# Attention work issued one product at a time between the large products, and one reciprocal per head

## The chip, the cores and the metric

The kernel runs on one core of one Trainium2 chip. The metric is the device time of one execution in microseconds (us). Several executions are timed, and one more is recorded by the hardware profiler.

## What is computed

Two transformer blocks on one sequence of 512 tokens with 1024 features, all in f32. The first block mixes sparse attention (8 heads of 64 in two groups; each has a selected, a window and a compressed branch) with retention (4 heads of 128). The second has an mLSTM layer (8 heads of 128) and a forgetting-attention layer (16 heads of 64), each with a convolutional feed-forward part.

```python
# sparse attention, one block of queries
sc = einsum('qghd,cgd->gqhc', qi, k_cmp) * scale
p_c = softmax(where(valid, sc, NEG));  o_c = einsum('gqhc,cgd->qghd', p_c, v_cmp)
p_s = softmax(where(smask, ss, NEG));  o_s = einsum('gqhk,gqkd->qghd', p_s, v_sel)
p_w = softmax(where(wmask, sw, NEG));  o_w = einsum('gqhk,kgd->qghd', p_w, v_win)
o = gi[..., 0:1] * o_c + gi[..., 1:2] * o_s + gi[..., 2:3] * o_w
# retention, one chunk
inner = einsum('bhnm,bhme->bhne', einsum('bhnd,bhmd->bhnm', qc, kc) * dmat, vc)
# mLSTM, one chunk
s = einsum('bhtd,bhsd->bhts', qt, kt) * exp(dmat - m_t[..., None])
num = einsum('bhts,bhse->bhte', s, vt) + ...
# forgetting attention
logits = einsum('bqhd,bkhd->bhqk', qi, k) + (ci[..., :, None] - c[..., None, :])
p = softmax(where(mask, logits, -inf));  o = einsum('bhqk,bkhd->bqhd', p, v)
```

All of it is causal. Around these stand the projections `h @ w_in`, `h @ w_up` and their like, whose weights are far larger than the activations.

## The kernel before

**Large products.** Each f32 operand of a projection is cut into a high and a low part, and `mm3` (L474) issues three products per weight tile of 128x128: high by high, high by low, low by high, mostly 512 columns wide. `gemm` and `gemm_tok` loop over the eight row blocks and call `mm3`, or issue the same three products themselves (L582 to L584). The weights come by DMA, are split by ScalarE (L169) and VectorE (L171), and are held in four buffers of each part.

**Attention as filling.** Four stages put attention work between the large products of a projection that does not depend on it: sparse attention, retention, mLSTM and forgetting attention. The work is written as generators. Each step issues some instructions and then yields a number, its written cost in ns. A filler holds a credit: `tick(ns)` after some large products adds `ns` times the stage's ratio, and steps are taken from the generator while the credit is above zero:

```python
    def tick(self, ns):
        self.credit += ns * self.ratio
        while self.gen is not None and self.credit > 0:
            try:
                self.credit -= next(self.gen)
...
def pipeline(items):
    n = len(items)
    for s in range(n + 2):
        yield from weave(*(items[s - d][d]() for d in range(3) if 0 <= s - d < n and items[s - d][d]))
```

An item is one head (of one branch). It has three parts, and in step `s` the pipeline weaves the first part of item `s`, the second of item `s - 1` and the third of item `s - 2`, one yield of each in turn; one such turn is called a round here. In the two softmax stages the parts are:

1. `score_steps` (L849): for each of four blocks of 128 queries, two score products of 128 to 512 columns into a bank of PSUM (the tile `s`, two buffers), with a mask product in the forgetting attention; then a reduction on VectorE (L862), the exponential with the row sum on ScalarE (L864), a reciprocal (L866) and a scaling (L868, L870) on VectorE. The result is a tile `P`.
2. `transpose_steps` (L874): ten transposes of 128x128 (L880), gathered in one bank (the tile `t`, one buffer) for each of four blocks of keys, and a copy by ScalarE (L882) to a tile `PT`.
3. `av` (L936, L1608), once for two heads: for each block of keys, the product of values and `PT` of either head (L939, L1613), 512, 384, 256 and 128 columns wide. The first head writes partitions 0 to 63 of the tile `o`, the second 64 to 127. The two products of one block are called a couple here.

The compressed branch has parts of the same kind with small tiles (`cmp_scores`, `cmp_transposes`, `avc`). Retention has `ret_scores`, `ret_out`, `ret_norm`, the mLSTM `m_scores`, `m_out`, `m_norm`; their products of weights and values have 128 output rows.

**What sets the order on each engine.** The framework's planner orders the whole program. Each engine gets, by the planner's own cost estimates, the instruction written earliest among those whose operands and buffers it deems ready. So the written order is a priority and not the order of execution: a later large product can run ahead of a transpose whose input isn't ready. On the chip each engine then keeps that order and waits on semaphores.

Of the kernel before, what the change touches and what calls it, by code (L numbers as in the profile page):

```python
# [194 lines left out]
def block_kernel(ctx: ExitStack, tc: tile.TileContext, I, out):  # L195
# [278 lines left out]
    def mm3(ps, w, a, first, last):  # L474
        (h, l), (ah, al) = w, a
        T.matmul(ps, lhsT=h, rhs=R(ah), start=first, stop=False)  # L476
        T.matmul(ps, lhsT=h, rhs=R(al), start=False, stop=False)  # L477
        T.matmul(ps, lhsT=l, rhs=R(ah), start=False, stop=last)  # L478

# [19 lines left out]
    def gemm(acts, nb, evac, lead=0, mid=None, halves=False, rest=None):  # L499
# [6 lines left out]
        b = 0  # L506
        if lead:
# [5 lines left out]
            for ts in thalf if halves else (slice(0, 512),):  # L513
                for k in range(KT):
                    for c in range(2 * lead):
                        mm3(ps[c][:, ts], cut(w[c // 2][k], c % 2), [t[:, ts] for t in acts[k]], k == 0, k == KT - 1)
                        if c % 2:
                            tick(1280)
# [6 lines left out]
        while b < nb:  # L525
            if KT <= 8:
                w = WT.get()
                for c in range(2):
                    ps = g_bank()
                    with in_order(tc, (mybir.EngineType.PE,)) if rest else nullcontext():  # L530
                        for k in range(KT):
                            mm3(ps, cut(w[k], c), acts[k], k == 0, k == KT - 1)
                            if k % 2:
                                tick(1280)
# [4 lines left out]
            else:  # L539
                ps = [g_bank(), g_bank()]  # L540
                for k0 in range(0, KT, 8):
                    w = WT.get()
                    for k in range(len(w)):
                        for c in range(2):
                            mm3(ps[c], cut(w[k], c), acts[k0 + k], k0 + k == 0, k0 + k == KT - 1)
                        tick(1280)
# [22 lines left out]
    def gemm_tok(acts, cols, evac, then=None, rest=None):  # L569
# [3 lines left out]
        with in_order(tc, (mybir.EngineType.PE,)) if rest else nullcontext():  # L573
            for k0 in (0, 4):
                w = WT.get()
                for k in range(4):
                    ah, al = acts[k0 + k]
                    h, l = w[k]
                    for i in range(4):
                        ts = slice(i * 128, (i + 1) * 128)  # L580
                        first, last = (k0 + k == 0), (k0 + k == 7)
                        T.matmul(ps[i][:, 0:cols], lhsT=R(ah)[:, ts], rhs=h, start=first, stop=False)  # L582
                        T.matmul(ps[i][:, 0:cols], lhsT=R(al)[:, ts], rhs=h, start=False, stop=False)  # L583
                        T.matmul(ps[i][:, 0:cols], lhsT=R(ah)[:, ts], rhs=l, start=False, stop=last)  # L584
                        if i % 2:
                            tick(1280)
# [235 lines left out]
    kcS = []  # L822
# [26 lines left out]
    def score_steps(P, g, q, k, cb, scale_cols):  # L849


        for i in range(4):
# [3 lines left out]
            T.matmul(ps[:, 0:L], lhsT=R(q[g][:, c]), rhs=R(k[0][g][:, 0:L]), start=True, stop=False)  # L856
            T.matmul(ps[:, 0:L], lhsT=R(q[g][:, c]), rhs=R(k[1][g][:, 0:L]), start=False, stop=cb is None)  # L857
            if cb is not None:
                T.matmul(ps[:, L - 128:L], lhsT=R(identr), rhs=R(maskr), start=False, stop=True)
            pr = unit("P")  # L860
            mx, rs = small(1, "mx"), small(1, "rs")
            V.tensor_tensor_reduce(out=pr[:, 0:L], in0=ps[:, 0:L], in1=cdiag[:, 512 - L:512] if cb is None else cb[:, 0:L],  # L862
                                   scale=1.0, scalar=3e38, op0=OP.add, op1=OP.min, accum_out=mx)
            A.activation(pr[:, 0:L], pr[:, 0:L], AF.Exp, scale=-1.0, bias=mx, accum_out=rs)  # L864
            rr = small(1, "rr")
            V.reciprocal(rr, rs)  # L866
            if scale_cols is None:
                V.tensor_scalar(pr[:, 0:L], pr[:, 0:L], rr, None, op0=OP.mult)  # L868
            else:
                V.tensor_scalar(pr[:, 0:L], pr[:, 0:L], rr, scale_cols[i], op0=OP.mult, op1=OP.mult)  # L870
            P.append(pr)
            yield 210 * (i + 1) + 60

    def transpose_steps(P, PT):  # L874

        yield from wait(1)
# [824 lines left out]
```

## Time and profile before

| | |
|---|---|
| three timed runs | 2171.95, 2175.36, 2176.06 us; median 2175.36 |
| the profiled execution | 2174.73 us, its span 2173.0 us |
| mean granted TensorE clock | 0.994 of full speed |
| busy: TensorE, its weight loads, VectorE, ScalarE, GpSimd | 97%, 79%, 57%, 43%, 16% of the span |
| the four stages, us from the span's start | sparse attention 97 to 271, retention 271 to 357, mLSTM 920 to 1026, forgetting attention 1564 to 1725 |

The span runs from the first to the last instruction of the profiled execution. In the rows, PE is TensorE's matmul, PEld its weight load, DVE VectorE, ACT ScalarE, POOL GpSimd, SP SyncE. `L880` is line 880 of the kernel. A record `t<-ident,P 128*128 128x128` writes the tile `t` from the tiles `ident` and `P`; the shape behind the names is that of the stationary operand, and the last one is the moving operand. Matmul records overlap, since they are pipelined, so what one costs is read from the step between starts. An f32 product with values has two records, one for each pass.

### The profile page before, as it was taken

The numbers are of one execution on the slowest core, as the hardware profiler recorded it, in microseconds if no ns is written. First come the engines' busy times: TensorE is split into PE (matmuls) and PEld (weight loads), VectorE is DVE, ScalarE is ACT, GpSimd is POOL, SyncE is SP. The second block draws the span as 40 slices with busy tenths as digits, with TensorE's granted clock in tenths as the row PEclk, the third lists the DMA queues.
The fourth block names the chain that finished last, engine by engine and source line by source line (L and its number), as shares of the span: only waits on it lengthen the run. The fifth ranks groups of instructions, "written<-read, shape, count | busy, mean of one in ns | idle before, by whom it ended". The sixth has DMA issues, their size and how long they took to land.

```text
span 2173.0 us, 26666 instructions
## 1 busy us (share of the span) xinstructions
PE 2116.9 (97%) x10314; PEld 1709.2 (79%) x10314; DVE 1240.5 (57%) x2247; ACT 943.2 (43%) x1638; POOL 341.0 (16%) x351
## 2 busy tenths in 40 slices
PE   7899999999999999999999999999999999999998
PEld 6766678887888888987888888889866788888887
DVE  7876545644333334867696664256477559666422
ACT  5666433344313424555364443234466536444322
POOL 5421000002101201320221110021121022111000
PEclk9999999999999999999999999999999999999999
DMA  6321122432233222422423332223322142333222
GB/s 162 106 77 58 40 63 82 128 97 78 97 97 93 89 90 79 134 91 73 131 78 97 97 97 87 80 87 126 118 70 66 57 129 78 97 97 97 88 74 72
DMA packets 242031, 198.75 MB, mean 91 GB/s; under 512 B 15182, under 2 KB 232986, under 8 KB 241904
## 3 DMA queue, kind: packets, MB, share of 16 engines
q1 hardware_dynamic: 237808, 186.11, 28.2%
q0 software_dynamic: 4096, 10.94, 1.6%
q8 instruction: 81, 1.33, 0.3%
q14 instruction: 46, 0.38, 0.1%
HBM read 190.69 MB, written 6.34 MB: 91 GB/s over the span
## 4 chain that ended last, share of the span: by engine, by line
PE 85%; DVE 5%; ACT 2%; issue 1%; DMA 0%; DVEq 0%; ACTq 0%; POOLq 0%; POOL 0%
PE g L476 24%; PE g L477 24%; PE g L478 24%; PE g L582 2%; PE g L584 2%; PE g L583 2%; PE t L880 1%; PE o L1613 1%; PE o L939 1%; PE s L856 1%; DVE wl L171 1%; PE s L857 1%; DVE x L1415 1%; PE t L1300 0%; PE o L1034 0%
## 5 line engine op out<-in xcount | busy, mean ns | idle before, releaser
L476 PE MATMUL g<-hi,wh 128*128 128x512 f32 (+1 forms) x2604 | 1005.4, 387 | 6.1 <-DVE gates L749 5.4
L477 PE MATMUL g<-lo,wh 128*128 128x512 f32 (+1 forms) x2604 | 994.9, 382 | 7.3 <-DVE lo L1420 7.3
L478 PE MATMUL g<-hi,wl 128*128 128x512 f32 (+1 forms) x2604 | 995.1, 382 | 3.6 <-POOL wl L171 1.9
L171 DVE TENSOR_TENSOR wl<-raw,wh 128x1024 fp32r<-128x1024 f32 (+4 forms) x337 | 405.5, 1205 | 399.4 <-ACT wh L169 398.6
L476 PEld LDWEIGHTS g<-hi,wh 128*128 128x128 f32 x2604 | 493.0, 190 | 115.4 <-issue 14.0
L169 ACT ACTIVATE wh<-raw 128x1024 fp32r<-128x1024 f32 (+3 forms) x348 | 355.9, 1025 | 521.8 <-PE g L477 452.6
L477 PEld LDWEIGHTS g<-lo,wh 128*128 128x128 f32 x2604 | 493.3, 189 | 104.5 <-DVE lo L1420 8.2
L478 PEld LDWEIGHTS g<-hi,wl 128*128 128x128 f32 x2604 | 493.2, 189 | 102.9 <-DVE wl L171 3.1
L864 ACT ACTIVATE P<-P,mx 128x128 f32<-128x128 f32 (+3 forms) x128 | 71.9, 561 | 47.4 <-DVE mx L862 46.1
L582 PE MATMUL g<-wh,hi 128*128 128x384 f32 (+3 forms) x256 | 85.4, 334 | 0.1
L584 PE MATMUL g<-wl,hi 128*128 128x384 f32 (+3 forms) x256 | 84.2, 329 | 0.0
L583 PE MATMUL g<-wh,lo 128*128 128x384 f32 (+3 forms) x256 | 84.1, 329 | 0.0
L882 ACT COPY PT<-t 128x512 f32<-128x512 f32 (+3 forms) x128 | 53.7, 420 | 53.4 <-PE t L880 52.4
L1133 POOL TENSOR_TENSOR relu<-relu 128x512 f32<-128x512 f32 x32 | 40.9, 1281 | 212.7 <-ACT relu L1132 207.5
L880 PE MATMUL t<-ident,P 128*128 128x128 f32 x320 | 65.2, 284 | 3.7 <-ACT PT L882 1.3
L880 PEld LDWEIGHTS t<-ident,P 128*128 128x128 f32 x320 | 38.7, 140 | 32.5 <-ACT PT L882 20.2
L1379 POOL TENSOR_TENSOR sq<-sq 128x512 f32<-128x512 f32 x16 | 27.1, 1694 | 229.4 <-ACT sq L1373 228.8
L374 DVE TENSOR_TENSOR lo<-relu,hi 128x512 fp32r<-128x512 f32 x32 | 21.9, 691 | 71.1 <-ACT hi L373 71.1
L582 PEld LDWEIGHTS g<-wh,hi 128*128 128x128 f32 x256 | 48.2, 188 | 4.4 <-issue 2.8
L454 POOL TENSOR_TENSOR sq<-sq 128x512 f32<-128x512 f32 x12 | 18.0, 1501 | 207.5 <-ACT sq L450 202.5
L866 DVE RECIPROCAL rr<-rs 128x1 f32<-128x1 f32 x128 | 20.5, 160 | 51.4 <-ACT P L864 50.9
L856 PE MATMUL s<-ks,qs 128*128 128x128 f32 (+3 forms) x128 | 46.9, 369 | 2.9 <-DVE mx L862 2.5
(926 smaller groups left out, 2222.4 us busy)
## 6 DMA issues: line engine op xcount, KB each, us to landing
raw<-in_ffn_w_up_dram SPq DMA_DIRECT2D x88, 512.0 KB, 4.9
raw<-in_w_in_dram SPq DMA_DIRECT2D x16, 1024.0 KB, 5.1
raw<-in_w_up_dram SPq DMA_DIRECT2D x16, 1024.0 KB, 5.4
raw<-in_w_down_dram SPq DMA_DIRECT2D x16, 1024.0 KB, 4.9
raw<-in_ffn_w_down_dram SPq DMA_DIRECT2D x12, 1024.0 KB, 5.0
raw<-in_mlstm_w_in_dram SPq DMA_DIRECT2D x8, 1024.0 KB, 5.3
raw<-in_fox_w_qg_dram SPq DMA_DIRECT2D x8, 1024.0 KB, 5.2
raw<-in_ffn_w_down_dram SPq DMA_DIRECT2D x6, 768.0 KB, 4.3
```

The lines of the kernel that those rows point to most:

```text
L169: self.nc.scalar.activation(h[:, 0:b - a].bitcast(F32R), raw[:, a:b], AF.Copy)
L171: e.tensor_tensor(l[:, 0:b - a].bitcast(F32R), raw[:, a:b], h[:, 0:b - a], op=OP.subtract)
L476: T.matmul(ps, lhsT=h, rhs=R(ah), start=first, stop=False)
L477: T.matmul(ps, lhsT=h, rhs=R(al), start=False, stop=False)
L478: T.matmul(ps, lhsT=l, rhs=R(ah), start=False, stop=last)
L582: T.matmul(ps[i][:, 0:cols], lhsT=R(ah)[:, ts], rhs=h, start=first, stop=False)
L583: T.matmul(ps[i][:, 0:cols], lhsT=R(al)[:, ts], rhs=h, start=False, stop=False)
L584: T.matmul(ps[i][:, 0:cols], lhsT=R(ah)[:, ts], rhs=l, start=False, stop=last)
L856: T.matmul(ps[:, 0:L], lhsT=R(q[g][:, c]), rhs=R(k[0][g][:, 0:L]), start=True, stop=False)
L864: A.activation(pr[:, 0:L], pr[:, 0:L], AF.Exp, scale=-1.0, bias=mx, accum_out=rs)
L880: T.transpose(pt[:, i * 128:(i + 1) * 128], P[i][:, j * 128:(j + 1) * 128], ident)
L882: A.copy(t[:, j * 128:512], pt[:, j * 128:512])
```

## The change

The credit is given after every single product of 512 columns, or in proportion for narrower ones, instead of after every six. Every step of the generators yields after nearly every product, with new written costs, and the four ratios are new. In `score_steps` the four row sums of a head go to one tile of four columns; one reciprocal serves all of them, the gate is multiplied into it in the sparse attention, and the four scalings follow at the end of the head. `transpose_steps` lets three rounds pass where it let one pass. The compressed branch's last part yields until the compressed values have been written (`vc_done`).

```diff
@@ -474,8 +474,11 @@
     def mm3(ps, w, a, first, last):
         (h, l), (ah, al) = w, a
         T.matmul(ps, lhsT=h, rhs=R(ah), start=first, stop=False)
+        tick(230)
         T.matmul(ps, lhsT=h, rhs=R(al), start=False, stop=False)
+        tick(230)
         T.matmul(ps, lhsT=l, rhs=R(ah), start=False, stop=last)
+        tick(230)
...
@@ -514,8 +517,6 @@
                 for k in range(KT):
                     for c in range(2 * lead):
                         mm3(ps[c][:, ts], cut(w[c // 2][k], c % 2), [t[:, ts] for t in acts[k]], k == 0, k == KT - 1)
-                        if c % 2:
-                            tick(1280)
...
-                            if k % 2:
-                                tick(1280)
...
-                        tick(1280)
...
-                        T.matmul(ps[i][:, 0:cols], lhsT=R(ah)[:, ts], rhs=h, start=first, stop=False)
-                        T.matmul(ps[i][:, 0:cols], lhsT=R(al)[:, ts], rhs=h, start=False, stop=False)
-                        T.matmul(ps[i][:, 0:cols], lhsT=R(ah)[:, ts], rhs=l, start=False, stop=last)
-                        if i % 2:
-                            tick(1280)
+                        for a, w_, f, e in ((ah, h, first, False), (al, h, False, False), (ah, l, False, last)):
+                            T.matmul(ps[i][:, 0:cols], lhsT=R(a)[:, ts], rhs=w_, start=f, stop=e)
+                            tick(0.45 * cols)
...
-    kcS = []
+    kcS, vc_done = [], []
...
+        rs = small(4, "rs")
         for i in range(4):
             L = 128 * (i + 1)
             ps = s_bank()
             c = slice(i * 128, (i + 1) * 128)
             T.matmul(ps[:, 0:L], lhsT=R(q[g][:, c]), rhs=R(k[0][g][:, 0:L]), start=True, stop=False)
+            yield 58 * (i + 1)
             T.matmul(ps[:, 0:L], lhsT=R(q[g][:, c]), rhs=R(k[1][g][:, 0:L]), start=False, stop=cb is None)
+            yield 58 * (i + 1)
             if cb is not None:
                 T.matmul(ps[:, L - 128:L], lhsT=R(identr), rhs=R(maskr), start=False, stop=True)
             pr = unit("P")
-            mx, rs = small(1, "mx"), small(1, "rs")
+            mx = small(1, "mx")
             V.tensor_tensor_reduce(out=pr[:, 0:L], in0=ps[:, 0:L], in1=cdiag[:, 512 - L:512] if cb is None else cb[:, 0:L],
                                    scale=1.0, scalar=3e38, op0=OP.add, op1=OP.min, accum_out=mx)
-            A.activation(pr[:, 0:L], pr[:, 0:L], AF.Exp, scale=-1.0, bias=mx, accum_out=rs)
-            rr = small(1, "rr")
-            V.reciprocal(rr, rs)
-            if scale_cols is None:
-                V.tensor_scalar(pr[:, 0:L], pr[:, 0:L], rr, None, op0=OP.mult)
-            else:
-                V.tensor_scalar(pr[:, 0:L], pr[:, 0:L], rr, scale_cols[i], op0=OP.mult, op1=OP.mult)
+            A.activation(pr[:, 0:L], pr[:, 0:L], AF.Exp, scale=-1.0, bias=mx, accum_out=rs[:, i:i + 1])
             P.append(pr)
-            yield 210 * (i + 1) + 60
+            yield 60
+        V.reciprocal(rs, rs)
+        if scale_cols is not None:
+            V.tensor_tensor(rs, rs, scale_cols, op=OP.mult)
+        for i in range(4):
+            V.tensor_scalar(P[i][:, 0:128 * (i + 1)], P[i][:, 0:128 * (i + 1)], rs[:, i:i + 1], None, op0=OP.mult)
...
     def transpose_steps(P, PT):
-        yield from wait(1)
+        yield from wait(3)
         for j in range(4):
             pt = t_bank()
             for i in range(j, 4):
                 T.transpose(pt[:, i * 128:(i + 1) * 128], P[i][:, j * 128:(j + 1) * 128], ident)
+                if i < 3:
+                    yield 60
             t = unit("PT")
             A.copy(t[:, j * 128:512], pt[:, j * 128:512])
             PT.append(t)
-            yield 107 * (4 - j)
+            yield 60
...
         for i in range(4):
             T.matmul(ps[:, i * 64:(i + 1) * 64], lhsT=R(qT[t][g][:, i * 128:(i + 1) * 128]), rhs=R(kcS[g]),
                      start=True, stop=True)
+            yield 50
...
-        yield 900
+        yield 50
...
         for i in range(4):
             T.transpose(pt[0:31, i * 128:(i + 1) * 128], P[0][:, i, :], ident)
+            yield 60
...
-        yield 430
+        yield 0
...
-                    cols = [gates[:, i, (t + 4 * g) * 3 + 1 + b:(t + 4 * g) * 3 + 2 + b] for i in range(4)]
+                    cols = gates[:, :, (t + 4 * g) * 3 + 1 + b]
...
@@ -939,7 +942,7 @@
                                 T.matmul(o_()[sp2[g_], j * 128:512],
                                          lhsT=vt[:, j * 128 + g_ * 64:j * 128 + g_ * 64 + 64],
                                          rhs=PTs[g_][j][:, j * 128:512], start=(b == 0 and j == 0), stop=False)
-                            yield 220 * (4 - j)
+                            yield 270 * (4 - j)
...
                 def avc(PTs=PTs, o_=o_):
+                    while not vc_done:
+                        yield 1000
                     for g_ in range(2):
                         T.matmul(o_()[sp2[g_], :], lhsT=vcmp[0:31, g_, :], rhs=PTs[g_][0][0:31, :],
                                  start=False, stop=True)
...
-    fill(nsa_gen(), 1.15)
+    fill(nsa_gen(), 0.85)
...
     gemm(hs, 1, lambda n, ps: r_evac(n + 2, ps))
     for _ in compress_out(next(cw), 1):
         pass
+    vc_done.append(True)
     gemm(hs, 2, lambda n, ps: r_evac(n + 4, ps))
...
-            yield 420 * (4 - j)
+            yield 216 * (4 - j)
...
             for j in range(i + 1):
                 T.matmul(po[:, c], lhsT=W[j][:, (i - j) * 128:(i - j + 1) * 128], rhs=rv[j][:, h * 128:(h + 1) * 128],
                          start=(j == 0), stop=(j == i))
+                yield 220
             A.activation(sq[:, c], po[:, c], AF.Square, scale=128.0 ** -0.5, accum_out=ss[:, i:i + 1])
-            yield 420 * (i + 1)
...
         for i in range(4):
             T.transpose(pt[:, i * 128:(i + 1) * 128], st[0][:, i * 128:(i + 1) * 128], ident)
+            yield 60
         V.tensor_tensor(rgT[h], rgT[h], pt, op=OP.mult)
         retT[h] = split(rgT[h], scale=0.5, tag="PT")
-        yield 900
...
-    fill(ret_gen(), 0.7)
+    fill(ret_gen(), 0.36)
...
                     mm3(pps[c][n], cut(w[4 * n + k], c), src[k], k == 0, k == 3)
-                    if c:
-                        tick(1280)
...
             T.matmul(ps[:, 0:n], lhsT=R(k[g][:, c]), rhs=R(q[g][:, j * 128:512]), start=True, stop=False)
+            yield 58 * (4 - j)
             T.matmul(ps[:, 0:n], lhsT=R(k[g][:, c]), rhs=R(ql[g][:, j * 128:512]), start=False, stop=True)
             V.tensor_tensor(dm[:, 0:n], ps[:, 0:n], dm[:, 0:n], op=OP.mult)
             st["dm"].append(dm)
-            yield 420 * (4 - j)
+            yield 58 * (4 - j)
...
             for j in range(i + 1):
                 T.matmul(b[:, c:c + 129], lhsT=st["dm"][j][:, (i - j) * 128:(i - j + 1) * 128], rhs=mv[j][h],
                          start=(j == 0), stop=(j == i))
+                if j < i:
+                    yield 220
             A.activation(sq[:, i * 128:(i + 1) * 128], b[:, c:c + 128], AF.Square, scale=128.0 ** -0.5,
                          accum_out=ss[:, i:i + 1])
             if i % 2:
                 V.tensor_scalar(u[:, i - 1:i + 1], b[:, 0:258].rearrange("p (i c) -> p i c", i=2)[:, :, 128],
                                 1e18, -1e18, op0=OP.min, op1=OP.max)
-            yield 420 * (i + 1)
+            yield 220
...
         for i in range(4):
             T.transpose(pt[:, i * 128:(i + 1) * 128], st["o"][:, i * 128:(i + 1) * 128], ident)
+            yield 60
         hm[h] = unit("hm")
         A.copy(hm[h], pt)
         m_done.add(h)
-        yield 900
...
-    fill(m_gen(), 1.5)
+    fill(m_gen(), 0.65)
...
-                        yield 220 * (4 - j)
+                        yield 270 * (4 - j)
...
-    fill(pipeline(fox_items()), 1.2)
+    fill(pipeline(fox_items()), 0.95)
```

## Rows read from the trace of the kernel before

**Rows 1.** The page, part 1: busy us (share of the span) and instructions of each engine.
```profile
PE 2116.9 (97%) x10314; PEld 1709.2 (79%) x10314; DVE 1240.5 (57%) x2247; ACT 943.2 (43%) x1638; POOL 341.0 (16%) x351
```

**Rows 2.** Windows of the four stages: length, busy us (instructions) by engine, clock, DMA.
```profile
core 0: us, PE busy (x) PEld busy (x) DVE busy (x) ACT busy (x) POOL busy (x), PEclk, DMA share, GB/s
97.00:271.00 174.00, 171.72 (x877) 116.10 (x874) 110.77 (x348) 100.91 (x250) 29.74 (x37) 0.99 0.20 61
271.00:357.00 86.00, 85.86 (x414) 69.22 (x413) 47.59 (x120) 31.40 (x68) 1.35 (x4) 1.00 0.21 65
...
920.00:1026.00 106.00, 100.14 (x558) 85.26 (x557) 74.03 (x220) 60.10 (x171) 17.73 (x20) 1.00 0.27 85
1564.00:1725.00 161.00, 156.02 (x775) 103.30 (x774) 113.41 (x329) 101.48 (x245) 30.77 (x44) 1.00 0.20 63
```

**Rows 3.** Waits of TensorE, whole span: us in total, times, longest.
```profile
PE s L1323 <- DVE mo L1318: 5.3, 8, 1.8
```

**Rows 4.** Timeline of TensorE from 157 us: start, duration, instruction.
```profile
157.74 0.27 PE L880 MATMUL t<-ident,P 128*128 128x128 f32 x1
...
158.09 0.40 PE L477 MATMUL g<-lo,wh 128*128 128x512 f32 x1
158.32 0.40 PE L856 MATMUL s<-ks,qs 128*128 128x512 f32 x1
158.55 0.39 PE L857 MATMUL s<-kl,qs 128*128 128x512 f32 x1
```

**Rows 5.** Timeline of TensorE from 430 us, transposes in a row (between: one large product).
```profile
430.28 0.60 PE L1099 MATMUL t<-ident,xi 128*128 128x128 f32 x4
...
430.95 0.40 PE L477 MATMUL g<-lo,wh 128*128 128x512 f32 x1
```

**Rows 6.** Timeline of TensorE from 203.5 us, two whole couples.
```profile
204.37 1.08 PE L939 MATMUL o<-PT,vs 128*64 128x512 f32 x4
205.38 0.39 PE L856 MATMUL s<-ks,qs 128*128 128x256 f32 x1
...
207.65 0.87 PE L939 MATMUL o<-PT,vs 128*64 128x384 f32 x4
208.45 0.44 PE L856 MATMUL s<-ks,qs 128*128 128x384 f32 x1
```

**Rows 7.** Timeline of TensorE from 211 us, a parted couple.
```profile
218.99 1.07 PE L939 MATMUL o<-PT,vw 128*64 128x512 f32 x2
219.99 0.33 PE L880 MATMUL t<-ident,P 128*128 128x128 f32 x1
220.25 1.07 PE L939 MATMUL o<-PT,vw 128*64 128x512 f32 x2
```

**Rows 8.** Timelines of TensorE, first and last lone 512-column product of the 19.
```profile
113.08 1.07 PE L939 MATMUL o<-PT,vs 128*64 128x512 f32 x2
...
1715.91 1.07 PE L1613 MATMUL o<-PT,fv 128*64 128x512 f32 x2
```

**Rows 9.** Groups of VectorE, the last one by shape: busy, mean ns, idle before, releaser.
```profile
L870 DVE TENSOR_SCALAR P<-P,rr,gates 128x128 f32<-128x128 f32 (+1 forms) x64 | 33.2, 518 | 0.4
L868 DVE TENSOR_SCALAR P<-P,rr 128x128 f32<-128x128 f32 (+1 forms) x64 | 25.4, 397 | 0.6
L866 DVE RECIPROCAL rr<-rs 128x1 f32<-128x1 f32 x128 | 20.5, 160 | 51.4 <-ACT P L864 50.9
...
L868 DVE TENSOR_SCALAR P<-P,rr 128x512 f32<-128x512 f32 x16 | 8.2, 515 | 0.4
```

**Rows 10.** Timeline of VectorE from 211 us, same head as rows 7.
```profile
215.23 0.54 DVE L870 TENSOR_SCALAR P<-P,rr,gates 128x512 f32<-128x512 f32 x1
...
217.40 0.17 DVE L903 TENSOR_TENSOR rs<-rs,gcmp 128x4 f32<-128x4 f32 x1
```

**Rows 11.** Timeline of TensorE from 160.1 us, score products of 128 columns.
```profile
161.34 0.31 PE L856 MATMUL s<-ks,qs 128*128 128x128 f32 x1
161.48 0.27 PE L857 MATMUL s<-kl,qs 128*128 128x128 f32 x1
```

## Prediction

> **What bounds the kernel now.** I read the page first, then the four stages that carry attention work, then TensorE's waits, and last the order of products inside a stage. In the busy times the reader is to see one engine that never rests: TensorE is busy 97% of the span, VectorE 57%, ScalarE 43% [rows 1]. The windows of the four stages (sparse attention, retention, mLSTM, forgetting attention: 527 us together) say the same of the part that the change touches. TensorE idles there for 2.28, 0.14, 5.86 and 4.98 us, 13.3 us in all [rows 2]. Its largest named wait is 5.3 us in eight pieces, the normalising transposes of the mLSTM behind VectorE [rows 3]. So an edit pays only if it takes work or exposed time off TensorE's queue, and what it saves on VectorE is hidden.
>
> Then the price of products on that queue. A record's duration overlaps the next one, so I take the step from one start to the next. A large product takes 0.23 us; a transpose alone between two large ones takes 158.09 − 157.74 − 0.23 = 0.12 us [rows 4]. Four transposes in a row take 430.95 − 430.28 − 0.23 = 0.44 us, 0.11 each [rows 5].
>
> The products of probabilities with values are dear. Each head's covers 64 of 128 output rows, and each is an f32 product of two passes. A 512-column one standing alone (x2) takes 219.99 − 218.99 = 1.00 us. Two heads' products back to back (x4) take 205.38 − 204.37 = 1.01 us, and a 384-column couple 0.80 [rows 6, 7]. The second head is free if nothing stands between. In rows 7 one transpose does: 1.00 us is paid again. I counted the two softmax stages: of 32 products of 512 columns, 19 stand alone, 8 in the first stage and 11 in the second; the first and the last are shown [rows 8]; of 32 with 384 columns, 8.
>
> **The change, part by part.**
>
> *VectorE work.* 128 reciprocals become 32: 96 × 0.160 = 15.4 us less. The first stage's scalings lose their second operand: 33.2 becomes 25.4, as the second stage's cost, 7.8 less [rows 9]. Sixteen small multiplies come in, 16 × 0.17 = 2.7 us [rows 10]. Net −20.5 us, hidden behind TensorE; I take 0 on the path. If the cover went, it could give at most these 20.5 us back.
>
> *Finer issue of full-width products.* Transposes cost 0.12 alone and 0.11 in a row [rows 4, 5], so over 320 of them this is 0 within 320 × 0.01 = 3 us. The value products of retention and mLSTM are f32 in two passes, 120 products; no row shows one alone. I take 0, and the transposes' 0.01 us on 240 passes bounds the loss at 2.4. The exception is the 128-column score product: it steps 0.14 where a 512-column one steps 0.23 [rows 4, 11], more than the quarter, 0.06, so something that large neighbours may hide is exposed. The two softmax stages have 128 of them, masks included, the mLSTM 16. If all fell to 0.06 that is 144 × 0.08 = 11.5 us; if they behave as transposes do, nothing. Both products of such a score fit into one large product's allowance (58 + 58 < 230 × 0.85), so they mostly stay neighbours. I take −1, with 0 and −11.5 as bounds.
>
> The Trainium skill ("TensorE: Matmul & The Clock Gate", section "Back-to-back issue gap") gives 81 ns for a sustained pair of weight load and 128-column matmul. By that, 144 such products could lose 0.14 − 0.08 = 0.06 us each, an estimated 8.6 us; the row's 0.14 and the transposes' indifference to isolation speak against getting it by order alone.
>
> *Coupled products.* Their order comes from the planner, which takes the earliest-written product that it deems ready. Two things bring them closer to the moment when their operands are ready. First, distance. From a second head's last score product to the first coupled product, the costs written before are 900 + 214 + 220 + 107, then a whole step of 2340 + 1070, sum 4851; over the ratio 1.15 and 1280 per six large products that is 19.8 large products. After, they are 232 + 60 + 3 × 60, then 1400 + 600, sum 2472; over 0.85 and 230 that is 12.6. Seven large products less are 7 × 0.23 = 1.7 us less slack. Second, lateness. All four scalings now follow the last exponential, so the 512-column tile waits for three shorter ones: (25.4 − 8.2) / 16 = 1.1 us later [rows 9]. In the example, the tile is scaled at 215.23 + 0.54 and its couple starts at 218.99 [rows 7, 10]: 3.2 us, which must hold four transposes and a copy, becomes 0.4. What is late next is the second head's transposes, and then its half of the couple.
>
> Against it stand two things. The next head's transposes now wait three rounds, so they stay out of the way while the four couples are issued. And VectorE spends 51.4 us in front of those 128 reciprocals, waiting for ScalarE [rows 9]; with 32 that stall shrinks and each exponential starts earlier.
>
> Bounds: if all 19 + 8 lone products were coupled, 9.5 × 1.00 + 4 × 0.79 = 12.7 us are gained (0.80 the row, 0.79 without its first step). If all now coupled were parted, the loss is 5 couples and 3 mixed ones of 512, 9 of 384, and the shorter ones. Columns scale the price by about 0.21 us per 128 (1.01 − 0.80, an estimate from rows 6), so 0.59 and 0.38 for 256 and 128; nearly all of those are coupled, so that makes 5 × 1.00 + 3 × 0.80 + 9 × 0.80 + 16 × 0.59 + 15 × 0.38 = 30 us. Slack shrinks at the first couple of each head pair, where only 5 of 16 are whole, and less behind it; I take four more partings at 1.00, +4 us.
>
> The skill's same page, Part 3 ("Packing small matmuls"), has products on different column groups run at once, about 4 ns apart. The trace agrees at 1.01 against 1.00 us; by it, too, every parting costs a whole product, which speaks against any issue order that parts them.
>
> *TensorE's idle time.* Bounds 0 to −13.3 us. The mLSTM wait hangs on a VectorE chain that the change leaves as it is (5.3 us stay). Of the remaining 8 I take half, −4, for the unblocked VectorE. On the other side a finer order may meet late operands more often; the mLSTM's 5.9 us, the worst stage now, bounds that at +6.
>
> *The guard on the compressed values* burns credit in lumps of 1000. Before the first such product the written costs are 2000 (compress), 5600 + 500 + 1400 (scores), 2880 (transposes), 5400 (couples): 17.8 thousand. The values come after 96 large products, 96 × 230 × 0.85 = 18.8 thousand. One or two lumps pass, in which large products run anyway: 0. No queue of SP or POOL is passed; the broadcast transfers start with their step as before.
>
> **Sum.** Span 2173.0; 0 − 1 + 4 − 4 = −1 gives 2172, plus 1.7 around the span (2174.73 − 2173.0): 2174. The profiled run lies 0.6 us below the median of the runs, 2175.36, so 2174 is taken for either. A change under 0.2% (4.3 us) can't be told from none.
>
> **The rivals.**
> 1. *Couples part (slower).* Place: the two softmax stages, where the slack of 3.2 us falls to 0.4. Price 1.00 or 0.80 us each. My other terms are −1 and −4, so from eleven extra partings on it decides (11 × 0.9 − 5 = 4.9 > 4.3). With fifteen it is 13.5 − 5 = +8.5: 2174.7 + 8.5 = 2183. For it: 11 of 16 first couples are parted or mixed already with more slack. Against: the three-round pause.
> 2. *Stalls go (faster).* Idle time falls by 10 of 13.3, couples stay: 2175 − 10 = 2165. For it: 51.4 us of VectorE stalls. Against: the largest wait isn't touched.
> 3. *Couples join (faster).* All lone ones meet: 2175 − 12.7 = 2162. For it: with the pause fewer older products are pending. Against: rows 7, where one older transpose was enough.
> 4. *Isolation hides what the narrow scores expose (faster).* 2175 − 9 = 2166. Against: transposes gain nothing so.
> 5. *New waits (slower).* The 5.9 us of the mLSTM stage a second time: 2181.
>
> **Chances.** No change that can be told, with 2174: 0.30. Rival 1: 0.26. Rival 2: 0.20. Rival 3: 0.13. Rival 4: 0.05. Rival 5: 0.06. So faster 0.38, same 0.30, slower 0.32. The range reaches to rivals 2 and 3 on one side and past rival 1 on the other, as more than fifteen partings are possible: 2160 to 2188. The forecast's own range is 2171 to 2179.
>
> **What would show it.** After, VectorE should be busy some 20 us less with 32 fewer-but-wider reciprocals, and TensorE's share unchanged. Lone (x2) 512-column products should be about 23 of 32; 30 would be rival 1, under 8 rival 3. Idle time in the four stages should be near 9 us; near 3 it is rival 2, above 17 rival 5. Transposes alone should still cost 0.11 to 0.12, and 128-column scores 0.14; near 0.06 it is rival 4. I am wrong if lone products move the other way than the time, or if retention and mLSTM, which have no couples, change by more than 3 us.

## The result, and the profile after

The changed kernel takes 2188.57 us (median of four runs, 2187.78 to 2190.14) against 2173.95 for the kernel before: ratio 1.0068, 95% interval 1.0051 to 1.0085. It is 14.6 us slower, where I had forecast no change that can be told. The profiled execution took 2189.26 us, its span 2187.6.

The busy times of the page, as [rows 1], look almost alike:

```profile
PE 2131.1 (97%) x10314; PEld 1707.8 (78%) x10314; DVE 1231.0 (56%) x2167; ACT 940.3 (43%) x1638; POOL 336.2 (15%) x351
```

TensorE issues the same 10314 products and is busy 14.2 us longer; that is nearly the whole loss. The windows of the four stages in this kernel (their ends lie up to some 17 large products off those of [rows 2], so they serve for the idle time; lengths at equal cuts stand in experiment 1):

```profile
core 0: us, PE busy (x) PEld busy (x) DVE busy (x) ACT busy (x) POOL busy (x), PEclk, DMA share, GB/s
97.00:279.70 182.70, 179.66 (x882) 116.05 (x882) 104.02 (x315) 100.68 (x250) 29.67 (x38) 0.99 0.18 58
279.70:366.00 86.30, 86.15 (x412) 68.01 (x411) 49.35 (x122) 32.38 (x70) 1.39 (x4) 1.00 0.19 63
926.00:1035.80 109.80, 103.99 (x573) 87.46 (x572) 74.95 (x220) 60.50 (x172) 16.93 (x21) 1.00 0.26 82
1573.50:1735.60 162.10, 156.52 (x757) 100.52 (x756) 107.90 (x278) 97.40 (x243) 27.80 (x44) 1.00 0.20 62
```

TensorE idles for 3.04, 0.15, 5.81 and 5.58 us, 14.6 in all, against 13.3: no idle time went away. Its largest wait in these stages, the mLSTM's, is the same 5.3 us as in [rows 3]:

```profile
PE s L1330 <- DVE mo L1325: 5.3, 7, 2.2
```

So the stages with softmax grew in busy time: at equal cuts from 253.64 to 262.23 us and from 147.55 to 151.63 (the first two fences of windows in experiment 1). TensorE's timeline in the forgetting attention shows how; one couple:

```profile
1606.48 1.07 PE L1620 MATMUL o<-PT,fv 128*64 128x512 f32 x2
1607.50 0.83 PE L879 MATMUL t<-ident,P 128*128 128x128 f32 x3
1608.09 0.48 PE L480 MATMUL g<-hi,wl 128*128 128x512 f32 x1
...
1609.67 0.52 PE L879 MATMUL t<-ident,P 128*128 128x128 f32 x3
1609.94 0.31 PE L859 MATMUL s<-maskr,identr 128*128 128x128 f32 x1
1610.09 0.27 PE L854 MATMUL s<-ks,qs 128*128 128x128 f32 x1
1610.29 1.07 PE L1620 MATMUL o<-PT,fv 128*64 128x512 f32 x2
```

The two heads' halves start 3.8 us apart. The first pays its full 1.0 us, and the second pays it again, where two together take 1.01 [rows 6]. By count, 23 of the 32 products of 512 columns stand alone, 19 before; of 384 columns 11, not 8; of 256 and 128 columns 10, not 3; and four of the compressed branch, none before. A couple that is parted leaves two lone products; counted by couples, 33 of 68 have another product between their two halves, 23 before, and of the 16 with 512 columns 14, before 11. Summed by their steps (first start to the start of what follows), half-width products take 69.4 us, not 63.3. They also begin at 92 places in the queue, not 77, and the large products beside such a place take longer. Here is one, in the sparse attention:

```profile
162.60 0.40 PE L478 MATMUL g<-lo,wh 128*128 128x512 f32 x1
162.84 0.40 PE L480 MATMUL g<-hi,wl 128*128 128x512 f32 x1
163.16 0.65 PE L942 MATMUL o<-PT,vs 128*64 128x256 f32 x4
163.75 0.50 PE L476 MATMUL g<-hi,wh 128*128 128x512 f32 x1
164.08 0.39 PE L478 MATMUL g<-lo,wh 128*128 128x512 f32 x1
```

Large products step 0.24 us (162.84 − 162.60). The one ahead of the couple steps 0.32, the one behind it 0.33: about 0.2 us for going in and coming out, an estimate from this one place. By this, 6.1 + 15 × 0.2 = 9.1 us of the 14.6 are partings; experiments 1 and 4 show that such sums come out too high.

Single small products cost what they cost in rows. A lone transpose, as in [rows 4]:

```profile
1614.53 0.39 PE L480 MATMUL g<-hi,wl 128*128 128x512 f32 x1
1614.76 0.27 PE L879 MATMUL t<-ident,P 128*128 128x128 f32 x1
1614.79 0.48 PE L476 MATMUL g<-hi,wh 128*128 128x512 f32 x1
1615.11 0.39 PE L478 MATMUL g<-lo,wh 128*128 128x512 f32 x1
```

Two large products and a transpose take 1615.11 − 1614.53 = 0.58 us, so the transpose costs 0.12. The large product ahead of it steps 0.23, the one behind it 0.32: of the two prices above only the one ahead is special to half-width products.

VectorE's groups, which answer to [rows 9], with the row maxima (L862) of this kernel and then, in a second fence, of the kernel before:

```profile
L871 DVE TENSOR_SCALAR P<-P,rs 128x128 f32<-128x128 f32 (+3 forms) x128 | 44.6, 411 | 0.9
L862 DVE CUSTOM_DVE_ANT_0 P<-s,cdiag 128x128 f32<-128x128 f32 (+1 forms) x64 | 30.9, 488 | 22.8 <-PE s L856 17.9 <-PE t L879 4.6
L862 DVE CUSTOM_DVE_ANT_0 P<-s,cb 128x128 f32<-128x128 f32 (+1 forms) x64 | 30.2, 487 | 18.2 <-PE s L859 13.2 <-DMA cb<-dC 4.4
...
L867 DVE RECIPROCAL rs<-rs 128x4 f32<-128x4 f32 x32 | 5.6, 175 | 13.8 <-ACT P L864 13.5
L869 DVE TENSOR_TENSOR rs<-rs,gates 128x4 f32<-128x4 f32 x16 | 4.3, 266 | 0.3
```

```profile
L862 DVE CUSTOM_DVE_ANT_0 P<-s,cb 128x128 f32<-128x128 f32 (+1 forms) x64 | 30.5, 476 | 2.9 <-PE s L859 2.1 <-DMA cb<-dC 0.7
L862 DVE CUSTOM_DVE_ANT_0 P<-s,cdiag 128x128 f32<-128x128 f32 (+1 forms) x64 | 30.4, 475 | 5.8 <-PE s L857 5.7
```

Scalings, reciprocals and multiplies fall from 79.1 to 54.5 us of busy time. The 44.6 us of the scalings count overlapping records once; by durations they are 128 × 0.411 = 52.6 us, and the fall is to 62.5. VectorE's wait ahead of the reciprocals falls from 51.4 to 13.8, but that ahead of the row maxima rises from 8.7 to 41.0. The stall moved to the place where VectorE waits, for the most part, for TensorE's scores (17.9 and 13.2 us of it); the 60.1 us became 54.8.

### The profile page after: what moved, and what is told of

The parts are those of the page before. It is cut to its first block, busy times and chain, and to the rows that moved or that the text cites. A ratio compares the mean times of both kernels' runs of the same rounds, so it can differ in the third digit from the quotient of the medians.

```text
span 2187.6 us, 26544 instructions
## 1 busy us (share of the span) xinstructions
PE 2131.1 (97%) x10314; PEld 1707.8 (78%) x10314; DVE 1231.0 (56%) x2167; ACT 940.3 (43%) x1638; POOL 336.2 (15%) x351
## 4 chain that ended last, share of the span: by engine, by line
PE 87%; DVE 7%; issue 2%; ACT 2%; DMA 1%; SPq 0%; POOL 0%; DVEq 0%; ACTq 0%; POOLq 0%
PE g L480 24%; PE g L478 24%; PE g L476 24%; PE g L581 5%; PE t L879 2%; PE o L942 1%; PE o L1620 1%; DVE wl L171 1%; PE s L854 1%; PE s L856 1%; DVE qs L386 1%; DVE x L1422 1%; PE t L1305 1%; DMA raw<-in_w_in_dram 0%; PE o L1040 0%
## 5 line engine op out<-in xcount | busy, mean ns | idle before, releaser
L879 PE MATMUL t<-ident,P 128*128 128x128 f32 x320 | 73.8, 286 | 4.8 <-ACT PT L883 1.7
L581 PEld LDWEIGHTS g<-wh,lo 128*128 128x128 f32 x256 | 48.2, 188 | 2.2 <-issue 1.2
L581 PEld LDWEIGHTS g<-wl,hi 128*128 128x128 f32 x256 | 48.2, 188 | 1.1
```

What stands on the lines that cost most here:

```text
L581: T.matmul(ps[i][:, 0:cols], lhsT=R(a)[:, ts], rhs=w_, start=f, stop=e)
L879: T.transpose(pt[:, i * 128:(i + 1) * 128], P[i][:, j * 128:(j + 1) * 128], ident)
```

## The experiments

All are compared with the kernel before, run on the same chip. Theory P: parted couples make the loss. Rivals: G, the grouped scalings make tiles late; F, the finer issue itself costs; and others named on the way.

**1. Couples whole, in both kernels.** The product of the head that comes last is written first, so the planner finds the partner ready when it takes it. The same edit stands in the three places where couples are written. It also turns the order of the two accumulations, which belong to different output rows.

```diff
-                            for g_ in range(2):
+                            for g_ in (1, 0):
                                 T.matmul(o_()[sp2[g_], j * 128:512],
```

> The changed kernel, with the two products of each couple written in the other order: the second head first, whose tile is the later one, so that the first head's tile is ready whenever the couple starts. In the planned order no half-width product then stands alone; before this edit 48 of the changed kernel's stand alone. Theory P (parted couples): the summed time of the couples falls from 68.7 to 47.6 us by 1.00, 0.79, 0.58 and 0.36 us for 512 to 128 columns, and there are 25 fewer places where half-width products begin and end, at about 0.2 us each, so the time falls by some 26 us, to about 2162. Rival N (the time is not won back, since TensorE then waits for something else): within 4 us of the changed kernel, 2185 to 2192. Rival F (the finer issue itself costs, by the many more alternations of large and small products): the couples' 26 us come off here too, but the same edit of the kernel before stays about 15 us below this one. Rival G (the grouped reciprocals make the tiles late): nothing in this run speaks for it, since the lateness only moves the couple.

> The kernel before, with the second head of each couple written first. In the planned order 4 half-width products stand alone, against 30 before the edit. Theory P: the couples' time falls from 62.4 to 49.0 us and there are 12 fewer places where they begin and end, 0.2 us each, so some 16 us less: about 2158, within 5 us of the changed kernel with the same edit. Rival N: within 4 us of the kernel before. Rival F: about 15 us under the changed kernel with the same edit.

Measured: changed kernel 2168.11 us, ratio 0.9971 (0.9960 to 0.9982); kernel before 2161.66, ratio 0.9946 (0.9929 to 0.9962), beside 2174.02. In the forgetting attention of the changed kernel with swapped heads:

```profile
1598.50 1.08 PE L1620 MATMUL o<-PT,fv 128*64 128x512 f32 x4
...
1601.22 0.87 PE L1620 MATMUL o<-PT,fv 128*64 128x384 f32 x4
...
1602.33 0.65 PE L1620 MATMUL o<-PT,fv 128*64 128x256 f32 x4
```

Couples are whole (x4); no 512-column product stands alone. The edit saves 20.5 us in the changed kernel (14.6 + 5.9) and 12.4 in the one before, both less than the 26 and 16 expected, so partings are 8.1 us of the 14.6. The intervals of the three ratios leave 5 to 6 us either way on that figure. Between the two kernels with swapped heads stay 6.5 us; that is short of rival F's 15, and more than the 5 that theory P allowed.

The two softmax stages say it again. Windows from large product 300 to 900 and 6280 to 6545, of the kernel before, then the changed one, then each with swapped heads, in four fences:

```profile
88.82:347.65 258.83, 253.64 (x1266) 181.37 (x1264) 158.39 (x454) 131.90 (x317) 34.49 (x43) 0.99 0.21 66
1570.84:1722.25 151.41, 147.55 (x739) 97.06 (x738) 104.04 (x316) 93.30 (x232) 27.24 (x41) 1.00 0.19 60
```

```profile
89.11:357.16 268.05, 262.23 (x1274) 180.49 (x1273) 153.50 (x425) 133.04 (x322) 34.33 (x43) 0.99 0.20 63
1580.74:1736.79 156.05, 151.63 (x736) 97.14 (x734) 101.81 (x267) 91.11 (x233) 24.14 (x40) 1.00 0.19 58
```

```profile
88.87:341.52 252.65, 247.99 (x1265) 179.38 (x1264) 157.04 (x453) 132.36 (x317) 33.63 (x43) 0.99 0.22 67
1561.00:1706.17 145.17, 139.47 (x738) 94.71 (x737) 104.30 (x316) 93.40 (x232) 26.79 (x41) 1.00 0.20 62
```

```profile
89.14:347.25 258.11, 251.09 (x1273) 178.54 (x1272) 155.07 (x426) 133.79 (x323) 34.30 (x43) 0.99 0.21 66
1571.53:1714.88 143.35, 139.68 (x735) 94.65 (x734) 100.80 (x267) 90.71 (x233) 25.95 (x40) 1.00 0.21 63
```

Swapping takes 6.2 + 6.2 us from the stages before and 9.9 + 12.7 after, a difference of 10.2, with the same granted clock in all four (0.99 and 1.00). Without partings the changed sparse attention is still 5.5 us longer, with 7.0 us of idle TensorE against 4.7; the forgetting attention is 1.8 us shorter.

**2. The grouped reciprocal, alone and undone.** In the kernel before, the four row sums share a tile, with one reciprocal and four scalings at the end of the head; in the changed kernel, each tile gets its own back.

```diff
+        V.reciprocal(rs, rs)
+        if scale_cols is not None:
+            V.tensor_tensor(rs, rs, scale_cols, op=OP.mult)
+        for i in range(4):
+            V.tensor_scalar(P[i][:, 0:128 * (i + 1)], P[i][:, 0:128 * (i + 1)], rs[:, i:i + 1], None, op0=OP.mult)
```

> The kernel before with the grouped reciprocal and the four scalings at the end of the head, and nothing else of the change. In the planned order the couples' time is 63.2 us against 62.4, with 2 more places where they begin. Theory P, with the distance in the written order and not the lateness as the cause of the parting: within 4 us of the kernel before. Rival G: most of the 14.6 us, 2182 or more. VectorE should be busy some 20 us less, which by all theories is hidden.

> The changed kernel with each tile's own reciprocal and scaling put back right behind its exponential. In the planned order the couples' time is 70.2 us against the changed kernel's 68.7, with 1 more place. Theory P with distance as the cause: 2188 to 2193, no better than the changed kernel. Rival G: back to 2174 to 2178.

Measured: alone 2173.89, ratio 1.0000 (0.9990 to 1.0009); undone 2190.47, ratio 1.0076 (1.0061 to 1.0091). G falls: the grouping neither costs nor gives. VectorE's busy time falls by 14.4 us in the first (1240.5 to 1226.1), where some 20 were expected, and rises by 7.5 in the second (1231.0 to 1238.5); TensorE hides both.

**3. The grain of the credit, alone and undone, with and without partings.** In the kernel before, a sixth of the credit after each large product; in the changed kernel, all of it after every sixth.

```diff
         T.matmul(ps, lhsT=h, rhs=R(ah), start=first, stop=False)
+        tick(1280 / 6)
...
-                            if k % 2:
-                                tick(1280)
```

```diff
+    held = [0, 0.0]
+
+    def tick6(ns):
+        held[0] += 1
+        held[1] += ns
+        if held[0] == 6:
+            tick(held[1])
+            held[:] = [0, 0.0]
...
-        tick(230)
+        tick6(230)
```

> Question: are the 6.5 us that stay between the two kernels with swapped heads (2161.7 and 2168.1) the price of issuing attention products one at a time? Here the kernel before, with swapped heads, gets its credit after every single large product, with its old steps and its old costs. In the planned order of the two softmax stages the half-width products are as in the kernel before with swapped heads (49.0 us, 70 places), but small products stand between large ones at 295 places, not 211; the changed kernel with swapped heads has 376. Theory F (each such place costs): 6.5 x 84 / 165 = 3.3 us, so 2165. Rival N (the places are free, the rest is new waits of the other edits): 2162.

> The same question from the other side: the changed kernel with swapped heads, its credit handed out only after every six large products. Half-width products as in the changed kernel with swapped heads (48.5 against 47.7 us, 67 places in both); places with small products between large ones: 239, not 376. Theory F: 6.5 x 137 / 165 = 5.4 us less than 2168, so 2163. Rival N: 2168, or more if six products' credit makes the chains later.

> The kernel before with nothing but the credit after every single large product. Planned half-width products 62.4 us as before, at 83 places, not 77. If partings set the time (theory P) and the finer credit is free: 2174 to 2175. With the price per place of theory F: 301 places, not 211, 3.5 us more: 2178. If finer credit parts couples on the chip as it does in the changed kernel: 2184 or more.

> The changed kernel with its credit after every six large products, all else as changed. If the finer credit were what parts the couples, they would come together here and the time would fall to 2174. Theory P by the planned order: half-width products 71.7 us at 94 places against 47.7 and 67 with swapped heads, (24.0 + 27 x 0.2) x 0.76 = 22.3 us above that kernel (0.76 is what swapping saved of the planned saving in the changed kernel, 20.5 of 26.8): 2168 + 22 = 2190, or 2163 + 22 = 2185 if theory F holds too. So the couples part by the new costs, ratios and pauses, not by the grain of the credit.

Measured: 2161.53, ratio 0.9936 (0.9923 to 0.9949); 2165.07, 0.9960 (0.9946 to 0.9974); 2176.01, 1.0003 (0.9993 to 1.0013); 2189.66, 1.0070 (1.0058 to 1.0082). The first and the third decide: attention products at 84 and 90 more places cost nothing, so F falls as a price per place. Undoing the grain gives at most some 2 us without partings (0.9960 against 0.9971, intervals overlap) and nothing with them. The grain doesn't part the couples either: 23 of 68 are parted in the third, as in the kernel before, and 35 in the fourth, 33 in the changed kernel.

**4. Couples parted in the kernel before.**

```diff
                                          rhs=PTs[g_][j][:, j * 128:512], start=(b == 0 and j == 0), stop=False)
-                            yield 220 * (4 - j)
+                                if not g_:
+                                    yield 110 * (4 - j)
+                            yield 110 * (4 - j)
```

> Couples parted in the kernel before by one thing alone: a yield between the two heads' products, with half the cost on either side. No product, no VectorE work, no credit and no ratio differs. In the planned order 24 of 32 products of 512 columns stand alone, not 19, and 13 of 384, not 8; the half-width products take 70.5 us by their steps, not 62.4, at 75 places, not 77. Theory P: (8.1 - 2 x 0.2) x 0.76 to 1.0 = 6 to 8 us more: 2180 to 2184. Rival W (partings cost little themselves, and go together with something else in the changed kernel): 2175.

Measured: 2179.72, ratio 1.0020 (1.0011 to 1.0029): 4.4 us more beside its own 2175.37, below the 6 to 8 expected, and far from nothing. Partings alone make the kernel slower; the steps summed in the trace (69.6 us, 63.3 before) overstate the price by some 30%, as they do for the swaps: in the changed kernel 69.4 − 48.0 and 25 places × 0.2 make 26.4 us, and 20.5 were measured.

**5. Which part of the change makes the loss.** The softmax stages' yields, costs, pause and ratios of before in the changed kernel, with and without swapped heads; and those of retention and mLSTM.

```diff
-        yield from wait(3)
+        yield from wait(1)
...
             PT.append(t)
-            yield 60
+            yield 107 * (4 - j)
...
-    fill(nsa_gen(), 0.85)
+    fill(nsa_gen(), 1.15)
```

> The changed kernel with the softmax stages' steps as before: yields, written costs, the one-round pause and the ratios 1.15 and 1.2. Kept are the credit after every product, the grouped reciprocal, the guard, and the new steps of retention and mLSTM. Planned half-width products 62.8 us at 85 places, not 68.7 at 92; nearly all of that in the forgetting attention (26.4, not 31.9), the sparse attention keeps its 36. Theory P: (5.9 + 7 x 0.2) x 0.76 = 5.5 us less than the changed kernel, 2183 to 2184. If these steps and costs are the whole cause: 2174 to 2176. If they are none of it: 2188 to 2190.

> Where do the 5 to 6.5 us come from by which the changed kernel with swapped heads stands above the kernel before with swapped heads, where no couple is parted in either? Here the softmax stages' steps, costs, pause and ratios of before are put back into the changed kernel with swapped heads. Theory S (the softmax steps, by new waits in the sparse attention): 2163 to 2164. Theory M (the steps of retention and mLSTM): 2168, as if nothing had been put back.

> The other half: the steps, costs and ratios of retention and mLSTM of before, put back into the changed kernel with swapped heads. Theory M: 2 us less, 2166, with the 1.9 us gone by which the large products 3600 to 3800 in the mLSTM take longer in every kernel of the changed family (51.8 against 49.9). Theory S: 2168.

Measured: 2183.07, ratio 1.0039 (1.0026 to 1.0052); 2164.54, 0.9945 (0.9933 to 0.9958); 2168.89, 0.9971 (0.9959 to 0.9983). The second equals the kernel before with swapped heads (0.9946): by the times the softmax stages' steps, not those of retention and mLSTM, hold the whole rest, 5.6 us with some 4 either way. Theory M, by which the second would have changed nothing, falls. Where in the kernel these 5.6 us lie the traces don't show: large products 300 to 900 take 259.4 us in the second run's profiled execution and 258.1 in the changed kernel with swapped heads, but the former has a stretch there, from 149.4 to 156.2 us, at a granted clock of 0.50, where the latter has 1.00. The first gave what P expected, about 6 us, nearly all in the forgetting attention:

```profile
89.20:356.76 267.56, 261.55 (x1273) 181.01 (x1272) 151.96 (x425) 132.07 (x322) 33.58 (x43) 0.99 0.20 64
1579.45:1727.09 147.64, 143.98 (x736) 95.10 (x734) 99.30 (x267) 91.16 (x233) 25.20 (x40) 1.00 0.20 61
```

The forgetting attention takes 147.64 us, not 156.05, with couples rejoined (4 of its 8 couples of 512 columns are parted, all 8 in the changed kernel), while the sparse attention stays at 267.56 and keeps its lone products: there all 8 are parted, 6 in the changed kernel.

**6. Which of these steps.** Whole steps in place of single products at the same sum of costs; and the one-round pause.

```diff
-            yield 58 * (i + 1)
             T.matmul(ps[:, 0:L], lhsT=R(q[g][:, c]), rhs=R(k[1][g][:, 0:L]), start=False, stop=cb is None)
-            yield 58 * (i + 1)
...
-            yield 60
+            yield 116 * (i + 1) + 60
```

> Of the gap between the two kernels with swapped heads, putting back the softmax steps as a whole took away about 4 us. Which part of them? Here only the yields between the products are taken out of the changed kernel with swapped heads: a score tile, a set of transposes and the compressed scores are whole steps again, at the sum of the new costs. Pause, ratios, credit and the costs of the couples stay new. Theory Y (woven product by product, each head's chain takes longer and something waits): 2163 to 2165. If it is the pause, the ratios or the costs: 2168.

> The changed kernel with swapped heads and the old pause of one round, not three, ahead of the transposes. Theory W (the pause): 2163 to 2165. If it is the yields or the ratios: 2168, or some us more, as the transposes now come before their tile is scaled.

> The changed kernel, heads not swapped, with whole steps in place of single products, as in the first of these three. In the planned order the half-width products take 70.7 us at 92 places (changed kernel 68.7 at 92). If the yields between products were what parts the couples, the planned order would have them together; it has not, so theory P gives 2189 to 2191, or 2185 to 2187 if theory Y holds as well.

Measured: 2163.48, ratio 0.9957 (0.9944 to 0.9969); 2168.17, 0.9972 (0.9963 to 0.9981); 2188.71, 1.0073 (1.0061 to 1.0086). The pause is nothing. Without partings whole steps give some 3 us (0.9957 against 0.9971, intervals overlap), as theory Y has it; with partings they give none, as P alone has it. The yields between products don't part the couples, and whether they cost by themselves is not settled.

## Why the prediction was wrong, step by step

*VectorE work*: right that it is hidden (experiment 2), too large in size. By durations the three groups fell by 16.6 us (79.1 to 62.5), not 20.5, and the engine's busy time only by 9.5, where the sign named was some 20.

*Finer issue of full-width products*: right that lone products cost no more, with transposes at 0.12 us and experiment 3. The 0.14 us of a 128-column score [rows 11] was read between two narrow products. Between two large ones it looks like this in the changed kernel:

```profile
1623.75 0.39 PE L478 MATMUL g<-lo,wh 128*128 128x512 f32 x1
1623.98 0.22 PE L859 MATMUL s<-maskr,identr 128*128 128x128 f32 x1
1624.04 0.45 PE L480 MATMUL g<-hi,wl 128*128 128x512 f32 x1
1624.32 0.40 PE L476 MATMUL g<-hi,wh 128*128 128x512 f32 x1
```

It steps 0.06, which was the sign of rival 4, but the large product behind it steps 0.28, so the two together cost 0.11 more than a large product alone. That is 0.03 less than 0.14 and not the 0.08 that rival 4 counted on, and the time did not fall. The estimate of 8.6 us from the Trainium skill's "TensorE: Matmul & The Clock Gate", section "Back-to-back issue gap", did not come either: order alone gained nothing in experiment 3 (1.0003). Wrong in the sum: with couples whole, the new softmax steps as a set still cost 5.6 us (0.9971 against 0.9945), where I had −1.

*Coupled products*: the direction came, and the size failed. I priced four more partings of 512 columns and nothing else. By couples there were three more of that width, and seven others: two of 384 columns, one of 256, two of 128, two of the compressed branch. And there were 15 more entries into half-width work, each at up to 0.2 us. Forecast +4, measured 8.1 by the swaps (9.1 by steps). The lone count came out at 23 of 32 as said, but in part by luck, since a parted couple leaves two lone products and four partings would have left up to 27. The direction was rival 1's, which asked for eleven partings at 0.9 us: there were ten, and they decided because the −1 and −4 set against them did not come. Its sign, 30 lone products of 512 columns, did not come. The reason was half right. In the changed kernel the second head's tile is copied too late for the first head's product in 13 of 16 first couples, before in 5 of 16. As the order is fixed when the kernel is built, this is how the planned order looks on the chip, and not by itself its cause. The lateness of the grouped scalings isn't the cause (experiment 2). Of the distance, experiment 5 shows that steps, costs, pause and ratios of before together rejoin couples in the forgetting attention; in the sparse attention they don't, and what parts them there stays open: grain, yields and grouping don't when undone one at a time.

*Idle time*: wrong, and with the −1 above the larger part of the miss. I took half of the 8 us that the mLSTM wait leaves, for VectorE's 51.4 us of stalls. It grew by 1.3, as the stall only moved to the row maxima, which mostly wait for TensorE itself. Some waits in the sparse attention are longer: with swapped heads the transposes of the compression (the tile `chid`) wait for VectorE twice, not once,

```profile
PE t L795 <- DVE chid L789: 3.2, 2, 2.3
PE t L879 <- DVE P L871: 1.2, 2, 1.0
PE g L480 <- DVE wl L171: 0.9, 1, 0.9
```

against, in the kernel before with swapped heads,

```profile
PE t L799 <- DVE chid L793: 2.3, 1, 2.3
PE t L880 <- DVE P L870: 1.1, 2, 0.6
PE g L478 <- DVE wl L171: 0.5, 1, 0.5
```

1.4 us more by these rows, a small piece of rival 5's new waits. They are no part of the 5.6 us, for with the softmax stages' old steps put back the first of them is longer still:

```profile
PE t L795 <- DVE chid L789: 4.3, 2, 2.3
```

*The guard*: 0 is in line with experiment 5, where it stays and the time is that of the kernel before with swapped heads. No run takes it out alone.

Retention and mLSTM kept within the 3 us named: 85.5 to 86.3 us between large products 652 and 934, and 171.1 to 172.2 between 3200 and 3800. Within the latter, products 3600 to 3800 take 51.8 us, not 49.9, since twelve records of mLSTM work (four of scores, eight of values) lie behind product 3600 in the changed kernel and ahead of it before.

The sum then: partings 8.1 in place of 4, and 6.5 in place of −1 − 4 for finer issue and idle time together, so 4.1 us of the miss are partings and 11.5 the rest. Of the 6.5 the softmax stages' new steps as a set hold 5.6; which of them, and by what, stays open. The fastest kernels are those of before with swapped heads, 2161.66, and with the single credit added, 2161.53: the change's grain does no harm, and what the kernel gained most by was whole couples.

## What to carry to other kernels

Where two narrow products run together at the price of one, count how many pairs stand whole in the order as built, and price every parted one of every width, and every entry. Count pairs and not lone halves, as one parted pair leaves two. A planner that takes what is ready in written order can part a pair whose early half is written first; here writing the late half first took the parted pairs from 23 to 2 and from 33 to none. A stall on an engine off the path that one edit removes is likely to turn up at the next thing the engine waits for.

## What the runs showed of the hardware beside this

A large product ahead of a half-width f32 product steps 0.32 us, ahead of a lone full-width transpose 0.23; behind either it steps 0.32 to 0.33. So about 0.1 us is the price of going into half-width work. Long runs of equal large products go at one of two steps, by stretch and kernel: 400 of them from number 4400 take 92.95 us in the kernel before and 93.33 in the changed one, and 1200 from number 2000 take 272.85 and 271.86; no cause was found, and it is 1 us either way. Among runs of one kernel the granted clock goes with the time, roughly: 2161.08 us at 0.995 and 2167.84 at 0.992 in the kernel with swapped heads and the old softmax steps, so two kernels that differ by 2 us need many runs.
